# No tile operation left to POOL in the second block's preparation, and the head norms' sums taken two columns later

## The chip, the core and the metric

The kernel runs on one core of a Trainium2 chip. The metric is the device time of one execution in microseconds (us), the median of three runs. The engines are PE (TensorE: matmuls, and PEld its weight loads), DVE (VectorE), ACT (ScalarE), POOL (GpSimd) and SP (SyncE, which here only issues DMAs). Each works through its own instructions in order and waits on semaphores for the others.

## The reference, cut to what matters

Two network blocks run on 512 tokens of width 1024. The first has a gated linear recurrence, a conformer convolution, cross attention and feed-forward layers. The second is where the change lies: a projection of the normalized input to 43 columns of 128 features, a bidirectional RWKV recurrence, attention over a neighbourhood, and a mixture of experts.

```python
h = rmsnorm(x, norm1_g[l])
p = h @ w_in[l]
p_rwkv, q, k, v, gate_logits = jnp.split(p, IN_SPLITS, axis=-1)
y_a = rwkv7_bidirectional(p_rwkv, ...) @ w_o_rwkv[l]
y_b = neighbourhood_attention_2d(q, k, v, ...) @ w_o_na[l]
...
# inside the recurrence
kk = kk * lax.rsqrt(jnp.sum(kk * kk, axis=-1, keepdims=True) + 1e-12)
k_f = heads(k * (1.0 + (a_f - 1.0) * k_a))
bonus = jnp.sum(r_h * (k_f + k_b) * r_k, axis=-1, keepdims=True) * v_h
# inside the attention, for q and for k
t32 * lax.rsqrt(jnp.mean(t32 * t32, axis=-1, keepdims=True) + RMS_EPS) * g
```

## The kernel before

**Products and weights.** A float32 product is made of three matmuls on fp32r parts (`mm3`, L524 to L526): high weight times high and low input, low weight times high input. The weights arrive as 1 MB tiles (`raw`), and `Stream.piece` splits a quarter tile at a time: ACT copies the high part to `whi` (L353), and another engine subtracts it from `raw` to give `wlo` (L356). One piece holds four blocks of 128 by 128, so twelve matmuls. There are eight `whi` and eight `wlo` buffers. In the first block L356 runs on DVE. In `second_mixer` the `rest` engine is POOL, and `LOV = (0, 2)` keeps pieces 0 and 2 of each tile on DVE, so every second piece goes to POOL.

**Columns.** `columns` makes the 43 columns in the order `W_IN`, each from 8 blocks, that is 24 matmuls into one accumulator (`acc`, five of them). DVE takes a column out of it: L1235 with L1237 and L1239 for the recurrence's columns (r, k, v), L1287 for the attention's q, k and v (columns 15 to 26), L1295 for the gates. For the four k columns of the recurrence (`sums`) and the eight q and k columns of the attention (`nsums`) `collect` squares the result on ACT (L1250), and four matmuls of PE add the squares up by head (`by_head`, L648), with a copy by ACT (L1260). That sum stands one column behind: after the first half (`begin`) of the next column.

**Preparation.** `prep` runs for the four pairs of heads p = 0 to 3. For each of the two directions d, `decay` (L1447 to L1463) makes decays with two matmuls, a scan on DVE (L1457) and exponentials on ACT (L1461, L1462). `products` then makes `kf` (ACT L1472, then L1474) and the tile `ab` of four products: L1477, L1478, L1483 and L1481, with L1480 ahead of the last. POOL has L1474 and L1477, DVE the others. `gram` is 16 small matmuls a half on `ab` (L1496). Between the two grams L1522 adds the two directions' `kf` on POOL. POOL also issues the DMAs of L1546.

**What sets the order.** The generators of `columns`, `prep` and `inverse` are drawn in turn by tables of digits (PREP, INVS, SOLVE and others), and a scheduler then lays each engine's instructions in one fixed order. `inverse(0)`, a forward substitution of 62 short DVE operations (L1568, L1571), is drawn among the preparation of p = 2 and 3, and `inverse(1)` behind it among the gates' columns (the solve stage). The recurrence itself (`chunk`) and the first output product follow in the chunk stage.

Of the kernel before, what the change touches and what calls it, by code (L numbers as in the profile page):

```python
# [8 lines left out]
F32 = mybir.dt.float32  # L9
# [17 lines left out]
E = 32  # L27
# [1 line left out]
TG, TN = 22, 8  # L29
QS = ('sync', 'gpsimd')  # L30
INV = 2
LOV = (0, 2)
AHD = 2
ENDS, ENDL = (), (3, 5, 6, 7)
PREP = "1011101111000230011101111011111111211112"
# [13 lines left out]
FETCH, LOOK, NP = 0, 8, 4  # L49
# [278 lines left out]
class Stream:  # L328
# [3 lines left out]
    def __init__(self, tc, pool, src, first=0):  # L332
        self.tc, self.nc, self.src = tc, tc.nc, src
        nc = tc.nc
        self.raws, self.parts = [(pool, 2)], [(pool, 2 * NP)]
        self.c, self.s, self.raw, self.got = first, 0, {}, {}
        self.queue, self.rest, self.byv = nc.sync, nc.vector, ()

    def fetch(self, c):
        if c not in self.raw and c < len(CHUNKS):  # L340
# [4 lines left out]
    def piece(self, h):  # L345
        if h in self.got or h >= NP * len(CHUNKS):
            return
        self.fetch(h // NP)
        n = 2048 // NP
        raw = self.raw[h // NP][:, h % NP * n:(h % NP + 1) * n]  # L350
        pool, bufs = self.parts[h % len(self.parts)]
        hi = pool.tile([P, n], F32R, name="whi", bufs=bufs)
        self.nc.scalar.copy(hi, raw)  # L353
        lo = pool.tile([P, n], F32R, name="wlo", bufs=bufs)
        rest = self.nc.vector if h % NP in self.byv else self.rest
        rest.tensor_sub(lo, raw, hi.bitcast(F32))  # L356
        self.got[h] = (hi, lo)

    def load(self, c):
# [85 lines left out]
class Kernel:  # L445
# [758 lines left out]
    def columns(self):  # L1204


        nc = self.nc
        R = self.R
        xs, rb = self.final_norm()
        for i in range(DT):  # L1210
            self.put(f"x{i}", self.x[i])
        c0 = R.tile([P, 15], F32, name="c0")
        nc.vector.tensor_add(c0, self.v("mu_prev_2", 0, 15), self.v("mu_next_2", 0, 15))
        nc.vector.tensor_scalar(c0, c0, -1.0, 1.0, op0=ALU.mult, op1=ALU.add)
        begun = {}

        def begin(m):

            if ("w_in_2", 0, 0, m) not in self.done:
                begun[m] = self.acc()  # L1220
                for k in range(4):
                    self.mm3(begun[m], self.st.block("w_in_2", 0, k, m), xs[k], k == 0, False)

        def col(m):
            if m not in begun:
                return self.dense(xs, "w_in_2", 0, range(8), m)
            for k in range(4, 8):
                self.mm3(begun[m], self.st.block("w_in_2", 0, k, m), xs[k], False, k == 7)
            return begun.pop(m)

        def shifted(m, dst):
            h, a = self.tmp(2), self.tmp()
            nc.vector.memset(h[:, 0:1], 0.0)
            nc.vector.memset(h[:, S + 1:S + 2], 0.0)
            nc.vector.tensor_mul(h[:, 1:S + 1], col(m), rb)  # L1235
            nc.scalar.activation(a, h[:, 1:S + 1], AF.Copy, scale=c0[:, m:m + 1])
            nc.vector.scalar_tensor_tensor(a, h[:, :S], self.v("mu_prev_2", m), a, op0=ALU.mult,  # L1237
                                           op1=ALU.add)
            nc.vector.scalar_tensor_tensor(dst, h[:, 2:], self.v("mu_next_2", m), a, op0=ALU.mult,  # L1239
                                           op1=ALU.add)  # L1240
            return dst

        kept = {}
        sums = R.tile([P, 64], F32, name="sums")
        self.nsums = self.B.tile([P, 128], F32, name="nsums")

        def collect(t, to, at, scale=1.0):

            sq = self.tmp()
            nc.scalar.activation(sq, t, AF.Square, scale=scale)  # L1250
            return sq, to, at

        def columns():
            late = None
            for m in W_IN:
                begin(m)
                if late:
                    sq, to, at = late
                    late = None
                    nc.scalar.copy(to[:, 8 * at:8 * at + 8], self.by_head(sq))  # L1260
                    if to is sums and at == 3:
                        self.rk = self.rsqrts(sums, 32, [(slice(0, 32), 1.0, 1e-12)])
                    elif at == 7:

                        self.rn = self.rsqrts(self.nsums, 64, [(slice(0, 32), 1.0, 64 * EPS),
                                                               (slice(32, 64), 1.0 / 64, EPS)])
                yield
                if m < 12:
                    n, i = "rkv"[m // 4], m % 4
                    at = i if n == "k" else 4 + "rv".index(n) + 2 * (i % 2)  # L1270
                    kept[n, i] = shifted(m, self.x[at])
                    if n == "k":
                        late = collect(kept[n, i], sums, i, self.v("k_k_2", i))
                elif m == 12:
                    w = shifted(m, self.tmp())
                    self.wl = R.tile([P, S], F32, name="wl")
                    nc.scalar.activation(self.wl, w, AF.Tanh)
                elif m == 13:
                    self.al = shifted(m, R.tile([P, S], F32, name="al"))
                elif m == 14:  # L1280
                    g = shifted(m, self.tmp())
                    nc.scalar.activation(g, g, AF.Tanh, scale=0.5)
                    nc.vector.tensor_scalar(g, g, 0.5, 0.5, op0=ALU.mult, op1=ALU.add)
                    self.put("gl", g, nc.scalar)
                elif m < 27:
                    t, ps = self.tmp(), col(m)
                    nc.vector.tensor_mul(t.rearrange("p (c r) -> p r c", r=8),  # L1287
                                         ps.rearrange("p (r c) -> p r c", r=8),
                                         rb.rearrange("p (r c) -> p r c", r=8))
                    self.put("n%s%d" % ("qkv"[(m - 15) // 4], (m - 15) % 4), t)  # L1290
                    if m < 23:
                        late = collect(t, self.nsums, m - 15)
                else:
                    t = self.tmp()
                    nc.vector.tensor_mul(t, col(m), rb)  # L1295

                    nc.scalar.activation(t, t, AF.Tanh, bias=self.hg[:, m - 27:m - 26], scale=0.5)
                    self.put(f"gate{m - 27}", t, nc.scalar)
                yield

        todo = columns()
        for _ in range(2 * W_IN.index(8) + 2):
            next(todo)
        inv = iter(())
        at = 0
        for p in range(4):
            for _ in self.prep(p, *(kept[x, p] for x in "krv")):
                for g, n in ((inv, INVS), (todo, PREP)):
                    for _ in range(int(n[at])):
                        next(g, None)  # L1310
                at += 1
            if p == 1:
                inv = self.inverse(0)
        for _ in inv:
            pass
        near = self.neighbours()
        for n, _ in enumerate(self.inverse(1)):
            for g, at in ((todo, SOLVE), (near, NEAR)):
                for _ in range(int(at[n])):
                    next(g, None)  # L1320
        return todo, near
# [102 lines left out]
    def prep(self, p, k, r, v):  # L1424

        nc = self.nc
        R, T, M = self.R, self.tmp, self.M
        rev = lambda t, d: t[:, ::-1] if d else t
        by = lambda t: t.rearrange("p (c s) -> p c s", s=64)
        lo, up = HALF  # L1430
# [11 lines left out]
        decays, rates, kd, abs_ = [], [], [], []  # L1442
# [24 lines left out]
        def products(d):  # L1467

            E, I = decays[d]
            ta = rates[d]  # L1470
            kf = T()
            nc.scalar.activation(kf, ta, AF.Identity, bias=self.ka[:, 4 + p:5 + p],  # L1472
                                 scale=self.ka[:, p:p + 1])
            nc.gpsimd.tensor_mul(kf, kf, k)  # L1474
            kd.append(kf)
            ab = self.B.tile([P, 8, 320], F32, name="ab", bufs=2)
            nc.gpsimd.tensor_mul(ab[:, :, 192:256], by(rev(r, d)), E[:, :, 1:])  # L1477
            nc.vector.scalar_tensor_tensor(ab[:, :, P:192], by(rev(kk, d)), -1.0, E[:, :, :64],  # L1478
                                           op0=ALU.mult, op1=ALU.mult)
            nc.vector.scalar_tensor_tensor(ta, ta, 1.0, kk, op0=ALU.add, op1=ALU.mult)  # L1480
# [38 lines left out]
        gram(0)  # L1519
        yield  # L1520
        rr = T()
        nc.gpsimd.tensor_add(rr, kd[0], kd[1])  # L1522
        nc.vector.scalar_tensor_tensor(rr, rr, self.v("r_k_2", p), r, op0=ALU.mult, op1=ALU.mult)
        yield
        gram(1)
# [7 lines left out]
        for d in range(2):  # L1533
# [7 lines left out]
            t = T()  # L1541
# [203 lines left out]

    def second_mixer(self):
        nc = self.nc
        self.st.queue, self.st.rest, self.st.byv = nc.sync, nc.gpsimd, LOV
        self.q1, self.q2 = (getattr(nc, q) for q in QS)
        with self.tc.tile_pool(name="systems", bufs=1) as G, \  # L1750
                self.tc.tile_pool(name="both", bufs=1) as self.B:
# [19 lines left out]
            with self.tc.tile_pool(name="chunks", bufs=1) as self.R:  # L1771
# [28 lines left out]
                    next(out)  # L1800
                for _ in out:
                    pass
        self.st.queue, self.st.rest = nc.sync, nc.vector
        for i in range(DT):
            self.get(f"x{i}", self.x[i])

# [414 lines left out]
```

## Time and profile before

| | us |
|---|---|
| median of three runs | 2491.69 (2486.46 to 2494.93) |
| the profiled execution's own time | 2489.94 |
| its span in the profile | 2488.1 |
| PE busy in the span | 2378.5 (96%) |
| DVE busy | 1399.0 (56%) |
| ACT busy | 938.6 (38%) |
| POOL busy | 454.9 (18%) |

The span is the time from the first to the last instruction of the profiled execution, and 1.8 us of its own time lie around it. Stretches are named by us from the span's start: the second block's columns begin at about 1530, `prep` runs from about 1604 to 1784, the solve stage to 1876, and the chunk stage to 2062. Matmuls are pipelined and the profile models their ends, so that PE is shown busy a little longer than it is: a wait of PE is better read from the idle time ahead of a row, and its speed from the distance of two starts.

### The profile page before, as it was taken

Reading aid. Unit: us, or ns where it says so; the run is one execution under the profiler, and the core shown is the slowest. Engines: PE = TensorE matmul, PEld = TensorE weight load, DVE = VectorE, ACT = ScalarE, POOL = GpSimd, SP = SyncE. Lnnn points to the kernel's source line nnn. Section 1 sums busy time; section 2 is a strip of 40 time slices with the busy share of each in tenths; the row PEclk is TensorE's granted clock in tenths of the full one; section 3 lists DMA queues with packets and bytes.
Section 4 is the critical chain, followed back from the end, with each engine's and each line's share of the span. In section 5 each row is a group of like instructions: output and inputs, shape, how many; then the busy total and the mean of one; then the engine's idle time right before and its main releaser. Section 6 shows DMA issues by size and latency. Waiting matters only on the chain. (4 is left out here: it accounts for less than half of the span.)

```text
span 2488.1 us, 34872 instructions
## 1 busy us (share of the span) xinstructions
PE 2378.5 (96%) x13357; PEld 1845.1 (74%) x13357; DVE 1399.0 (56%) x2639; ACT 938.6 (38%) x1706; POOL 454.9 (18%) x428
## 2 busy tenths in 40 slices
PE   7999999999999999999999999988999989999996
PEld 6887788888888779888888888766876666764442
DVE  7998666545454546565645455669465776631110
ACT  4666444333243235444424244454243322321110
POOL 2012101101011000101101013344223221402211
PEclk8999999999999998999999999999898989989999
DMA  4332212222332213213222223355653434479998
GB/s 176 119 127 93 88 63 92 102 96 90 102 106 89 93 52 136 85 60 102 93 94 102 102 87 113 117 153 146 179 165 119 132 111 144 135 264 365 379 377 293
DMA packets 131197, 344.53 MB, mean 138 GB/s; under 512 B 40435, under 2 KB 66834, under 8 KB 101328
## 3 DMA queue, kind: packets, MB, share of 16 engines
q1 hardware_dynamic: 122944, 327.29, 38.2%
q0 software_dynamic: 5632, 10.49, 2.3%
q10 hardware_dynamic: 2448, 4.46, 0.5%
q8 instruction: 107, 1.75, 0.3%
q14 instruction: 66, 0.54, 0.1%
HBM read 307.33 MB, written 34.87 MB: 138 GB/s over the span
## 5 line engine op out<-in xcount | busy, mean ns | idle before, releaser
L524 PE MATMUL acc<-xn,whi 128*128 128x512 f32 x1656 | 660.9, 399 | 12.7 <-ACT xn L562 6.6
L353 ACT CAST whi<-raw 128x512 fp32r<-128x512 f32 x652 | 398.2, 620 | 708.0 <-PE acc L525 597.1
L526 PE MATMUL acc<-xn,wlo 128*128 128x512 f32 x1656 | 653.2, 395 | 1.6 <-DVE wlo L356 1.6
L525 PE MATMUL acc<-xn,whi 128*128 128x512 f32 x1656 | 654.0, 395 | 0.0
L356 DVE TENSOR_TENSOR wlo<-raw,whi 128x512 fp32r<-128x512 f32 x605 | 448.2, 746 | 294.6 <-ACT whi L353 292.5
L524 PEld LDWEIGHTS acc<-xn,whi 128*128 128x128 f32 x1656 | 314.9, 190 | 84.4 <-ACT xn L562 6.6
L526 PEld LDWEIGHTS acc<-xn,wlo 128*128 128x128 f32 x1656 | 314.4, 190 | 69.6 <-DVE wlo L356 2.4
L525 PEld LDWEIGHTS acc<-xn,whi 128*128 128x128 f32 x1656 | 315.2, 190 | 68.1 <-issue 3.4
L524 PE MATMUL acc<-act,whi 128*128 128x512 f32 (+1 forms) x676 | 252.9, 375 | 3.0 <-DVE tmp L1817 1.7
L525 PE MATMUL acc<-act,whi 128*128 128x512 f32 (+1 forms) x676 | 252.7, 374 | 2.6 <-DVE act L560 2.6
L526 PE MATMUL acc<-act,wlo 128*128 128x512 f32 (+1 forms) x676 | 252.8, 374 | 0.0
L723 POOL TENSOR_TENSOR tmp<-tmp 128x512 f32<-128x512 f32 x48 | 74.4, 1549 | 622.8 <-DVE tmp L721 555.7
L582 POOL TENSOR_TENSOR tmp<-tmp 128x512 f32<-128x512 f32 x56 | 80.6, 1440 | 421.7 <-ACT tmp L575 401.9
L524 PEld LDWEIGHTS acc<-act,whi 128*128 128x128 f32 x676 | 130.0, 192 | 25.8 <-DVE tmp L1817 2.2
L525 PEld LDWEIGHTS acc<-act,whi 128*128 128x128 f32 x676 | 130.2, 193 | 25.2 <-DVE act L560 3.0
L526 PEld LDWEIGHTS acc<-act,wlo 128*128 128x128 f32 x676 | 130.1, 192 | 21.9
L560 DVE TENSOR_TENSOR act<-tmp,act 128x512 fp32r<-128x512 f32 x88 | 61.1, 694 | 89.4 <-ACT act L559 87.5
L559 ACT CAST act<-tmp 128x512 fp32r<-128x512 f32 x88 | 54.3, 620 | 122.1 <-POOL tmp L723 91.3
L2099 POOL DMA_INDIRECT out<-tmp,tid x32 | 50.7, 1583 | 245.0 <-ACT tmp L2098 155.4
L356 POOL TENSOR_TENSOR wlo<-raw,whi 128x512 fp32r<-128x512 f32 x47 | 66.7, 1422 | 133.3 <-ACT whi L353 105.0
L703 DVE SCALAR_TENSOR_TENSOR tmp<-tmp,vec 128x512 f32<-128x512 f32 x96 | 72.2, 752 | 17.0 <-ACT tmp L700 15.3
L2067 PE MATMUL acc<-raw,xn 128*64 128x512 f32 x320 | 75.8, 602 | 4.3 <-DMA raw<-wex 4.2
(439 smaller groups left out, 3290.4 us busy)
## 6 DMA issues: line engine op xcount, KB each, us to landing
raw<-wst SPq DMA_DIRECT2D x162, 1024.0 KB, 5.0
raw<-wex SPq DMA_DIRECT2D x56, 1024.0 KB, 16.5
whi<-wex SPq DMA_DIRECT2D x56, 256.0 KB, 6.5
wlo<-wex SPq DMA_DIRECT2D x56, 256.0 KB, 6.3
x<-wex SPq DMA_DIRECT2D x12, 1024.0 KB, 9.6
bkv<-bkv SPq DMA_DIRECT2D x32, 192.0 KB, 2.7
rec<-ab SPq DMA_DIRECT2D x8, 512.0 KB, 3.2
sp_gate<-tmp ACTq DMA_DIRECT2D x16, 256.0 KB, 2.6
```

The source lines that it names most:

```text
L353: self.nc.scalar.copy(hi, raw)
L356: rest.tensor_sub(lo, raw, hi.bitcast(F32))
L524: nc.tensor.matmul(ps, w[0], x[0], start=first, stop=False)
L525: nc.tensor.matmul(ps, w[0], x[1], start=False, stop=False)
L526: nc.tensor.matmul(ps, w[1], x[0], start=False, stop=last)
L559: nc.scalar.copy(h, src)
L560: nc.vector.tensor_sub(lo, src, h.bitcast(F32))
L582: nc.gpsimd.tensor_add(n, accs.pop(), t)
L703: nc.vector.scalar_tensor_tensor(z, h[:, k:k + S], taps[k], y, op0=ALU.mult, op1=ALU.add)
L723: nc.gpsimd.tensor_mul(z, u, ge)
L2067: nc.tensor.matmul(pg[a], h[:, o:o + SLOTS], w[2 * k + n], start=c + k == 0, stop=c + k == 4)
L2099: nc.gpsimd.indirect_dma_start(out=self.out[hf], out_offset=bass.IndirectOffsetOnAxis(ap=tid[:, i:i + 1], axis=0), in_=y, in_offset=None, ...
```

## The change

The split of every weight piece, both products of POOL in `products` and the sum of the two `kf` go to DVE. The table LOV and the switch of engines in `Stream` go. The list `late` in `columns` now holds up to two entries: sums of the recurrence's k columns are still taken behind the next column, and those of the attention's q and k when a second one is waiting, or beyond column 22.

```diff
@@ class Stream
-        self.queue, self.rest, self.byv = nc.sync, nc.vector, ()
+        self.queue = nc.sync
...
-        rest = self.nc.vector if h % NP in self.byv else self.rest
-        rest.tensor_sub(lo, raw, hi.bitcast(F32))
+        self.nc.vector.tensor_sub(lo, raw, hi.bitcast(F32))
@@ columns
-            late = None
+            late = []
             for m in W_IN:
                 begin(m)
-                if late:
-                    sq, to, at = late
-                    late = None
+                if late and (late[0][1] is sums or len(late) > 1 or m > 22):
+                    sq, to, at = late.pop(0)
                     nc.scalar.copy(to[:, 8 * at:8 * at + 8], self.by_head(sq))
...
-                        late = collect(kept[n, i], sums, i, self.v("k_k_2", i))
+                        late.append(collect(kept[n, i], sums, i, self.v("k_k_2", i)))
...
-                        late = collect(t, self.nsums, m - 15)
+                        late.append(collect(t, self.nsums, m - 15))
@@ prep
-            nc.gpsimd.tensor_mul(kf, kf, k)
+            nc.vector.tensor_mul(kf, kf, k)
...
-            nc.gpsimd.tensor_mul(ab[:, :, 192:256], by(rev(r, d)), E[:, :, 1:])
+            nc.vector.tensor_mul(ab[:, :, 192:256], by(rev(r, d)), E[:, :, 1:])
...
-        nc.gpsimd.tensor_add(rr, kd[0], kd[1])
+        nc.vector.tensor_add(rr, kd[0], kd[1])
@@ second_mixer
-        self.st.queue, self.st.rest, self.st.byv = nc.sync, nc.gpsimd, LOV
+        self.st.queue = nc.sync
```

Line numbers fall by one to three in the changed kernel: L356 becomes L354, L648 L646, L1287 L1284, L1474 L1471, L1477 L1474, L1478 L1475, L1480 L1477, L1481 L1478, L1483 L1480, L1496 L1493.

On DVE, in `products` for p = 1, from the weight piece that stands in the scan's place to the end of the first direction's products, this is the order before:

```order
L356 TENSOR_TENSOR wlo<-raw,whi 128x512
L1457 SCALAR_TENSOR_TENSOR tmp<-cst,tmp 128x512
L1460 MEMSET tmp 128x8
L1478 SCALAR_TENSOR_TENSOR ab<-tmp 128x8x64 x2
L1480 SCALAR_TENSOR_TENSOR tmp<-tmp 128x512
L1483 TENSOR_TENSOR ab<-tmp 128x8x64
L1481 SCALAR_TENSOR_TENSOR ab<-tmp 128x8x64
```

And this is the same stretch now:

```order
L354 TENSOR_TENSOR wlo<-raw,whi 128x512
L1474 TENSOR_TENSOR ab<-x_106,tmp 128x8x64
L1475 SCALAR_TENSOR_TENSOR ab<-tmp 128x8x64
L1471 TENSOR_TENSOR tmp<-tmp,x_99 128x512
L1477 SCALAR_TENSOR_TENSOR tmp<-tmp 128x512
L1480 TENSOR_TENSOR ab<-tmp 128x8x64
L1478 SCALAR_TENSOR_TENSOR ab<-tmp 128x8x64
```

The scan and the first direction's L1474 and L1475 now stand ahead of these rows; in all, the first gram of p = 1 has two L1474 and one L1471 more ahead of it on DVE.

On PE, in the preparation of p = 2, the third of the attention's sums (its square is tmp_14096) stands here before, followed by the first gram:

```order
L524 MATMUL acc_14114<-xn_12758,whi_14041 128x512
L525 MATMUL acc_14114<-xn_12759,whi_14041 128x512
L526 MATMUL acc_14114<-xn_12758,wlo_14043 128x512
L648 MATMUL aux_14131<-cst_80,tmp_14096 128x2 x4
L1496 MATMUL aux_14137<-ab_14060 64x64
```

In the changed kernel the second sum (of tmp_13814) stands in that place, with four matmuls of the column between it and the gram:

```order
L522 MATMUL acc_14108<-xn_12758,whi_14035 128x512
L523 MATMUL acc_14108<-xn_12759,whi_14035 128x512
L524 MATMUL acc_14108<-xn_12758,wlo_14037 128x512
L646 MATMUL aux_14125<-cst_80,tmp_13814 128x2 x4
L522 MATMUL acc_14108<-xn_12762,whi_14071 128x512
L523 MATMUL acc_14108<-xn_12763,whi_14071 128x512
L524 MATMUL acc_14108<-xn_12762,wlo_14073 128x512
L522 MATMUL acc_14108<-xn_12766,whi_14071 128x512
L1493 MATMUL aux_14131<-ab_14054 64x64
```

The third sum moved to the place that the fourth has before, a column of 24 matmuls later; each of the eight has moved to the place of the next one in this way. Ahead of the first gram itself PE has, from the first decay matmul of its pair, 46, 34, 26 and 49 column matmuls for p = 0 to 3, where it had 44, 24, 29 and 38.

On DVE, in the same preparation, the column out of which that third square is made (L1287) stands behind the products of the first direction before, with the rows of the substitution (z, NT) between:

```order
L1478 SCALAR_TENSOR_TENSOR ab_14101<-tmp_13979,tmp_14029 128x8x64
L1568 TENSOR_TENSOR z_14070<-X_13996,NT_13997 128x135
L1480 SCALAR_TENSOR_TENSOR tmp_13986<-tmp_13986,tmp_13979 128x512
L1483 TENSOR_TENSOR ab_14060<-tmp_14057,tmp_13989 128x8x64
L1481 SCALAR_TENSOR_TENSOR ab_14060<-tmp_13986,tmp_13989 128x8x64
L1571 TENSOR_TENSOR NT_13997<-NT_13997,z_14070 128x5x27
L1287 TENSOR_TENSOR tmp_14076<-acc_14040,rb_13012 128x8x64
```

Now it stands ahead of them:

```order
L1284 TENSOR_TENSOR tmp_14070<-acc_14034,rb_13012 128x8x64
L1568 TENSOR_TENSOR NT_13991<-NT_13991,z_14031 128x4x28
L1471 TENSOR_TENSOR tmp_14051<-tmp_14051,x0_99 128x512
L1477 SCALAR_TENSOR_TENSOR tmp_13980<-tmp_13980,tmp_13973 128x512
L1480 TENSOR_TENSOR ab_14054<-tmp_14051,tmp_13983 128x8x64
L1478 SCALAR_TENSOR_TENSOR ab_14054<-tmp_13980,tmp_13983 128x8x64
```

So the column leaves its accumulator before the first direction's products, and these now hold L1471 as a row of DVE's own.

## Rows read from the trace of the kernel before

**Rows 1.** Stretches: us, then busy time (and instructions) by engine, PEclk, DMA.
```profile
1604.00:1639.00 35.00, 31.41 (x194) 23.07 (x193) 26.80 (x55) 20.23 (x38) 15.38 (x14) 0.95 0.51 125
1639.00:1681.00 42.00, 35.80 (x209) 27.47 (x209) 25.51 (x38) 19.16 (x37) 19.07 (x21) 0.92 0.55 152
1681.00:1725.00 44.00, 38.71 (x224) 29.58 (x224) 40.82 (x70) 18.79 (x38) 19.79 (x18) 0.88 0.48 119
1725.00:1784.00 59.00, 55.18 (x350) 43.30 (x349) 35.86 (x64) 17.36 (x36) 13.29 (x9) 0.94 0.72 203
1784.00:1876.00 92.00, 88.03 (x782) 72.22 (x780) 59.52 (x131) 36.29 (x72) 25.32 (x29) 0.87 0.49 148
1876.00:2062.00 186.00, 171.43 (x2136) 121.49 (x2137) 126.37 (x406) 58.05 (x182) 56.58 (x128) 0.94 0.38 119
```
**Rows 2.** Waits of PE, 1600 to 1784: us in total, times, longest us.
```profile
PE aux L648 <- ACT tmp L1250: 9.1, 2, 5.3
PE aux L1496 <- DVE ab L1481: 8.7, 2, 6.2
PE aux L660 <- DVE tmp L1460: 1.1, 1, 1.1
```
**Rows 3.** PE in order of time: start, us, instruction, [idle before <- what ended it].
```profile
1655.74 1.97 PE L1496 MATMUL aux<-ab 64*64 64x64 f32 x32 [6.20 <-DVE ab L1481]
...
1659.08 0.63 PE L524 MATMUL acc<-xn,whi 128*128 128x512 f32 x1
...
1659.51 0.63 PE L525 MATMUL acc<-xn,whi 128*128 128x512 f32 x1
...
1663.52 0.39 PE L524 MATMUL acc<-xn,whi 128*128 128x512 f32 x1
...
1663.75 0.39 PE L525 MATMUL acc<-xn,whi 128*128 128x512 f32 x1
...
1698.37 1.87 PE L648 MATMUL aux<-cst,tmp 128*128 128x2 f32 x8 [5.29 <-ACT tmp L1250]
```
**Rows 4.** DVE in order of time, in the products of p = 1.
```profile
1644.25 0.73 DVE L1510 SCALAR_TENSOR_TENSOR tmp<-x,vec,aux 128x512 f32<-128x512 f32 x1
...
1645.23 1.68 DVE L356 TENSOR_TENSOR wlo<-raw,whi 128x512 fp32r<-128x512 f32 x1
...
1649.46 1.57 DVE L1480 SCALAR_TENSOR_TENSOR tmp<-tmp 128x512 f32<-128x512 f32 x1
1652.19 1.73 DVE L1483 TENSOR_TENSOR ab<-tmp 128x512 f32<-128x512 f32 x1 [1.16 <-POOL tmp L1474]
1653.85 1.75 DVE L1481 SCALAR_TENSOR_TENSOR ab<-tmp 128x512 f32<-128x512 f32 x1
1655.51 0.68 DVE L1480 SCALAR_TENSOR_TENSOR tmp<-tmp 128x512 f32<-128x512 f32 x1
1656.12 0.68 DVE L1483 TENSOR_TENSOR ab<-tmp 128x512 f32<-128x512 f32 x1
```
**Rows 5.** POOL in order of time, in the same stretch.
```profile
1650.44 2.94 POOL L1474 TENSOR_TENSOR tmp<-tmp,x 128x512 f32<-128x512 f32 x2
1653.34 1.71 POOL L356 TENSOR_TENSOR wlo<-raw,whi 128x512 fp32r<-128x512 f32 x1
```
**Rows 6.** DVE in order of time, in the preparation of p = 2.
```profile
1685.09 0.74 DVE L1510 SCALAR_TENSOR_TENSOR tmp<-x,vec,aux 128x512 f32<-128x512 f32 x1
...
1690.84 1.68 DVE L356 TENSOR_TENSOR wlo<-raw,whi 128x512 fp32r<-128x512 f32 x1
...
1696.53 1.06 DVE L1287 TENSOR_TENSOR tmp<-acc,rb 128x512 f32<-128x512 f32 x1
```
**Rows 7.** Waits of PE, 1530 to 1606.
```profile
PE aux L592 <- POOL tmp L582: 1.1, 1, 1.1
```
**Rows 8.** Groups of instructions by line, POOL, 1530 to 2130: count | busy us, mean ns | idle before.
```profile
L356 POOL TENSOR_TENSOR wlo<-raw,whi 128x512 fp32r<-128x512 f32 x47 | 66.7, 1422 | 133.3 <-ACT whi L353 105.0 <-issue 12.3 <-PE acc L526 10.8
```
**Rows 9.** Waits of ACT, 1530 to 2130.
```profile
ACT whi L353 <- PE acc L525: 79.9, 44, 8.0
```

More of the change, by code (lines that the diff above doesn't have):

```diff
@@ L31 @@
 INV = 2
-LOV = (0, 2)
 AHD = 2
@@ L1802, in second_mixer @@
                     pass
-        self.st.queue, self.st.rest = nc.sync, nc.vector
+        self.st.queue = nc.sync
         for i in range(DT):
```

## The prediction

> **What bounds the kernel now.** I read the stretches first. PE is the bound nearly everywhere, but in the preparation it has holes: 31.41 of 35 us busy, 35.80 of 42, 38.71 of 44 and 55.18 of 59 in the four pairs' stretches, and there the granted clock falls to 0.95, 0.92, 0.88 and 0.94 [rows 1]. Next, the waits of PE say who makes the holes: 9.1 us in two waits of L648 for a square of ACT, and 8.7 us in two waits of a gram (L1496) for the last product of DVE; the longest are 5.3 and 6.2, so the others are 3.8 and 2.5, together 17.8 us [rows 2]. The square itself waits for DVE's L1287, so all four are DVE being late. Then the clock: after the 6.20 us wait two matmuls start 0.43 us apart, a little later 0.23 us [rows 3]; these are the levels of 1.2 and 2.4 GHz. In the four stretches (1 - clock) times length is 1.75 + 3.36 + 5.28 + 3.54 = 13.9 us, so 27.9 us at the low level. About 5 us of these lay inside the waits themselves (my reading of 3.0 in the third, and less in the others); the rest costs (0.43 - 0.23) / 0.43 of itself, 10.6 us at most. I take 9, since the small matmuls of the grams do not double. The preparation thus loses some 27 us on PE.
>
> Last, why DVE is late. In the products of p = 1 one and the same operation takes 1.57, 1.73 and 1.75 us while POOL is at L1474 and L356, and 0.68 just after, when POOL is idle; L1483 also stands idle for 1.16 us until POOL's L1474 is done [rows 4, 5]. So a DVE operation on two tiles of SBUF loses about 1.0 us to a POOL operation beside it. The Trainium skill (page SBUF — State Buffer, section Who interferes with whom) has a DVE instruction with two SBUF inputs and a GpSimd instruction that reads SBUF exclude each other, so that the second waits for the whole of the first; the trace agrees in kind, with 1.75 us against 0.68.
>
> **The change, part by part.** *Work moved.* POOL has 47 weight splits of 1422 ns [rows 8]; by the code 8 + 8 products and 4 sums come with them. On DVE each costs the distance of two starts, 1656.12 - 1655.51 = 0.61 us [rows 4]: 67 x 0.61 = 40.9 us more DVE work, spread from 1530 to 2062. In the preparation it is 36 of them (16 splits and all 20 others), 22 us. Against that stand the 1.0 us stretches, which go wherever DVE was busy beside POOL.
>
> *Second pair (wait of 6.2).* From L1510 at 1644.25 to the end of the last product at 1655.60 DVE took 11.35 us [rows 4]. Without POOL it loses 1.00 (L356), 0.89 (L1480), 1.16 (the wait), 1.05 (L1483) and 1.07 (L1481), 5.17 in all; the order adds two L1474 and one L1471, 1.83. It ends 3.3 us earlier, at 1652.25. PE was there at 1655.74 - 6.20 = 1649.54 [rows 3] and has ten matmuls more ahead of the gram now (34 against 24), 2.27 us: 1651.8. The wait left is 0.45.
>
> *First pair (2.5).* The same count: three stretched products back (about 3), one product added (0.6), two matmuls more (0.45). 0.3 is left.
>
> *Third pair (5.3).* The sum is now a column later, 24 x 0.227 = 5.4 us of PE work, and its column is taken out ahead of the products, so its wait goes altogether. What is late next is the first gram, which stood right behind. PE would be there at 1698.37 - 5.29 = 1693.08 [rows 3], less three matmuls (26 against 29) plus the sum's own work, about 1693.3. DVE before had done the products just ahead of L1287 at 1696.53 [rows 6]. Four rows between 1685.09 and there are stretched by about 1.0 each (the split at 1690.84 is one [rows 6]); L1474, L1471 and L1287 (0.9) come in ahead and one L1478 goes. That is 1696.4 - 4.1 + 1.5 = 1693.8 at best; the substitution's rows stand among them and may be hit, so I take 1695. The wait left is 1.5, and 0.5 at the second gram: 2.
>
> *Fourth pair (3.8).* Again the sum's wait goes. DVE's run to the first products holds three operations more and the substitution's middle rows; PE has 11 matmuls more ahead (49 against 38), 2.5 us. DVE is the slower here by my count of the order with the distances above, by about 3 us.
>
> So 17.8 becomes 0.3 + 0.45 + 2 + 3, about 5.8: 12.0 us back. Of the clock's 9 I leave 3, since waits of 2 to 3 us may again be followed by a low clock, as the 2.5 us one was (0.95 in its stretch [rows 1]): 6 back. The wait for rk (L660, 1.1 [rows 2]) stays.
>
> *Columns before the preparation.* PE waits 1.1 us for the last sum of the norm on POOL [rows 7]; two splits that stood among those sums are gone from POOL, so this goes: 1.0 back.
>
> *Splits as a wait.* A split on DVE can stand behind a run of products. But ACT's L353 waits 79.9 us in 44 times for PE's L525 to free a buffer [rows 9]: the pieces are made as far ahead as eight buffers allow, and one piece is 12 x 0.227 = 2.7 us of PE work. A delay of 10 us is covered; with a run of products of over 15 us it would not be.
>
> *Solve and chunk stage.* 12 and 8 splits move there, 7.3 and 4.9 us of DVE. In the solve stage PE is busy 88.03 of 92 [rows 1] and the stretches lost offset the new work; in the chunk stage DVE is on the recurrence's path, but POOL, which also copies and scales state there, loses 8 pieces of 1.4. Bounds: 2 us gained, and 5 lost (all eight on the path). I take 1 lost, near the middle.
>
> Sum: -12.0 - 6 - 1.0 + 1 = -18 us on the profiled execution's 2489.94, that is 2472. The median of the runs is 1.75 higher, so the forecast is 2474.
>
> **The rivals.** *All waits go.* If the scheduler's order meets the products in time in the third and fourth pair too, 17.8 + 9 + 1.1 come back, -28: 2464. For it: DVE's 40.82 of 44 us in the third pair are swollen by the stretches [rows 1]. Against: the grams there stand early in PE's order.
>
> *The wait comes back at the grams.* DVE is busy 40.82 of 44 us there already, and gets 22 us of work in the preparation. If the stretches are only half as large as I read them, some 10 us of it are net, and they lie ahead of grams. The sums' waits then go (9.1), the grams' grow by about as much, and the clock gains 2 or 3 less: -6 instead of -18, 2486. The Trainium skill (page Perfetto Trace Analysis, section Optimizing Scalar/DVE Operations) speaks for this one: with DVE saturated it would move work off it, though it adds that DVE and GpSimd share a read port, so that this might not help; the rows of the trace bear out the second half.
>
> *Slower: DVE becomes the bound.* If POOL's operations took their time in the shadow of DVE's own waits, so that the stretches bring back under 10 us, DVE runs 12 us or more behind at the end of the preparation. It then carries this into the solve stage, where the splits (12 of them) lie in one queue with 62 dependent rows of `inverse(1)`: pieces come late, PE waits for `wlo`, and the clock, 0.87 there already [rows 1], falls further. 12 for the backlog and 5 for the chunk stage, less 8 for sums and front, is +9: 2501. It decides when DVE in the stretches of the preparation is busy without a gap; it had 2 to 23 us of gaps in each [rows 1].
>
> *No effect.* The sums one column later are no use if their squares are later by as much. With L1287 ahead of the products in the order, I hold this for covered by the case of the grams.
>
> **How the numbers follow.** Forecast 2474 (from 2466 to 2481): 0.56. All waits gone, 2464: 0.17. Waits back at the grams, 2486: 0.20. Slower, 2501: 0.07. A measurement of this kernel tells about 0.3%, 7.5 us, from no change. Faster by more than that, under 2484, is the first two and a fifth of the third: 0.77; within it, the rest of the third: 0.16; slower 0.07. The range leaves out the slower case and a part of the fastest: 2462 to 2488.
>
> **What would show it.** Right: no operation of DVE on 128x512 tiles over about 1.1 us between 1604 and the gates; DVE busy in the four preparation stretches about as long as before, in spite of 36 more operations; L648 gone from PE's waits; the waits of L1496 under 6 us together and now in p = 2 and 3; granted clock over 0.95 in the third stretch; the solve stage some 20 us earlier. Wrong: PE waiting for `wlo`, or for L1496 by more than 10 us, or a preparation (L1447 of p = 0 to the last L1540) that is not at least 12 us shorter. A longer chunk stage than 186 us by over 5 would show that the splits lie on the recurrence's path.

## The result and the profile after

| | before | after |
|---|---|---|
| median of the runs (4 each) | 2489.07 us (2483.7 to 2494.93) | 2453.38 us (2450.2 to 2466.59) |
| the profiled execution's own time | 2489.94 | 2453.04 |
| its span | 2488.1 | 2451.3 |

The ratio is 0.986, with a 95% interval of 0.984 to 0.988: 35.7 us less by the medians, 36.9 by the two profiled executions. The forecast was 18 less, 2474, with a range of 2462 to 2488. The sign and the mechanism were right; the size was half of what came, and the range did not hold the time.

The first lines of the page of the changed kernel:

```profile
span 2451.3 us, 34809 instructions
...
PE 2359.5 (96%) x13357; PEld 1830.2 (75%) x13357; DVE 1403.8 (57%) x2706; ACT 938.1 (38%) x1706; POOL 359.6 (15%) x361
```

DVE has 67 operations more than before (2706 against 2639) and is busy only 4.8 us longer (1403.8 against 1399.0). POOL has 67 fewer and is busy 95 us less.

**Where the 36.8 us of span lie.** I followed single instructions of PE through both traces. The 7201st matmul stands in the columns ahead of the first wait that differs: it starts at 1560.0 us before and at 1553.6 after. These 6.4 us lie in work that the change does not touch. In the profiled executions of the kernels below, which all share that work, the same matmul starts at 1552.1 to 1560.0, so the 6.4 are scatter, and the execution of before was at its late end. (With one profile of each kernel, whether the medians' 35.7 hold more than the 32.2 and this scatter cannot be told.) From that matmul to the first L1646 of the recurrence (L1643 now), through the rest of the columns, the preparation and the solve stage, before took 316.4 us and after 284.2: **32.2 us less**. From there to the end it is 1.8 us more. This middle stretch holds 1963 or 1964 instructions of PE in every kernel, and I use it below to compare them. These are its busy times by engine, in the kernel before and then in the changed one (columns as in [rows 1]):

```profile
1560.00:1876.40 316.40, 290.64 (x1964) 230.46 (x1962) 217.64 (x418) 127.68 (x245) 107.56 (x100) 0.92 0.53 152
```

```profile
1553.60:1837.80 284.20, 280.97 (x1963) 223.40 (x1961) 211.81 (x471) 127.84 (x245) 26.22 (x44) 0.95 0.58 168
```

DVE does 53 operations more in 5.8 us less. Idle time of PE, the stretch less PE's busy time, was 25.8 us and is 3.2. The time at the low level of the clock, 2 x (1 - clock) x length, was 51 us and is 28. The four stretches of the preparation and the solve and chunk stages, which answer to [rows 1], are:

```profile
1595.60:1624.00 28.40, 28.28 (x182) 20.40 (x181) 26.86 (x64) 19.64 (x36) 0.78 (x1) 1.00 0.51 125
1624.00:1659.20 35.20, 34.94 (x215) 26.24 (x214) 26.99 (x52) 19.58 (x37) 9.47 (x16) 1.00 0.79 219
1659.20:1697.20 38.00, 37.81 (x247) 28.06 (x245) 34.91 (x77) 21.43 (x44) 4.91 (x8) 1.00 0.62 166
1697.20:1746.00 48.80, 48.80 (x332) 39.49 (x329) 31.36 (x74) 14.42 (x30) 0.00 (x0) 1.00 0.77 210
1746.00:1837.40 91.40, 89.15 (x782) 73.50 (x781) 60.84 (x144) 37.13 (x72) 7.31 (x16) 0.85 0.49 151
1837.40:2023.20 185.80, 168.83 (x2139) 119.63 (x2140) 131.38 (x412) 58.01 (x182) 47.58 (x120) 0.96 0.39 120
```

In the preparation PE now has no hole to speak of, and its clock is granted in full: the 0.95, 0.92, 0.88 and 0.94 of before are 1.00 four times. The waits of PE within the middle stretch, which answer to [rows 2] and [rows 7] (us in total, times, longest):

```profile
PE aux L1396 <- ACT tmp L1391: 1.4, 2, 0.7
PE aux L1493 <- DVE ab L1478: 0.5, 2, 0.3
```

The 17.8 us of [rows 2] for the sums and the grams have become 0.5, and the wait for rk and those ahead of the preparation are gone. The first line is the solve stage's. Not listed is the wait that ends the stretch, ahead of the first L1643: it is 1.3 us, and was 1.4.

This is DVE in the products of p = 1, which answers to [rows 4]:

```profile
1629.49 0.75 DVE L1507 SCALAR_TENSOR_TENSOR tmp<-x,vec,aux 128x512 f32<-128x512 f32 x1 [0.95 <-DMA bkv<-tmp]
...
1634.94 0.69 DVE L1471 TENSOR_TENSOR tmp<-tmp,x 128x512 f32<-128x512 f32 x1
1635.54 0.69 DVE L1477 SCALAR_TENSOR_TENSOR tmp<-tmp 128x512 f32<-128x512 f32 x1
1636.14 0.69 DVE L1480 TENSOR_TENSOR ab<-tmp 128x512 f32<-128x512 f32 x1
1636.74 0.68 DVE L1478 SCALAR_TENSOR_TENSOR ab<-tmp 128x512 f32<-128x512 f32 x1
```

Every product takes 0.68 or 0.69 us, where [rows 4] has 1.57 to 1.75, and they follow each other at 0.60. From the start of L1507 (L1510 before) to the end of the last product it is 7.93 us, against 11.35.

### The profile page after: what moved, and what is told of

It is laid out like the page before. It is cut to its first block, busy times and chain, and to the rows that moved or that the text cites. A ratio compares the mean times of both kernels' runs of the same rounds, so it can differ in the third digit from the quotient of the medians.

```text
span 2451.3 us, 34809 instructions
## 1 busy us (share of the span) xinstructions
PE 2359.5 (96%) x13357; PEld 1830.2 (75%) x13357; DVE 1403.8 (57%) x2706; ACT 938.1 (38%) x1706; POOL 359.6 (15%) x361
## 3 DMA queue, kind: packets, MB, share of 16 engines
q8 instruction: 107, 1.75, 0.3%
## 5 line engine op out<-in xcount | busy, mean ns | idle before, releaser
L354 DVE TENSOR_TENSOR wlo<-raw,whi 128x512 fp32r<-128x512 f32 x652 | 479.9, 742 | 307.3 <-ACT whi L352 304.3
L701 DVE SCALAR_TENSOR_TENSOR tmp<-tmp,vec 128x512 f32<-128x512 f32 x96 | 72.2, 752 | 17.0 <-ACT tmp L698 15.3
L684 DVE TENSOR_TENSOR x<-x,acc 128x512 f32<-128x512 f32 x80 | 52.2, 681 | 39.5 <-PE acc L524 39.5
```

The lines of the kernel that those rows point to most:

```text
L354: self.nc.vector.tensor_sub(lo, raw, hi.bitcast(F32))
L684: self.nc.vector.tensor_add(self.x[m], self.x[m], ps)
L701: nc.vector.scalar_tensor_tensor(z, h[:, k:k + S], taps[k], y, op0=ALU.mult, op1=ALU.add)
```

## The experiments

The theory (A) was that DVE came late because an operation of it on two SBUF tiles is held up by a POOL operation beside it, and that the rest followed from that. The first four kernels take the change apart, the next three put POOL or DVE work back without any use, and the last one tries the same step elsewhere.

| kernel | median, us | ratio to before (95%) | middle stretch, us | PE idle in it, us | low clock in it, us |
|---|---|---|---|---|---|
| before | 2489 | | 316.4 | 25.8 | 51 |
| after | 2453.38 | 0.984 to 0.988 | 284.2 | 3.2 | 28 |
| e1_move: engines only | 2452.18 | 0.983 to 0.987 | 283.8 | 3.1 | 28 |
| e2_late: sums only | 2489.06 | 0.998 to 1.002 | 317.9 | 28.4 | 48 |
| e3_splits: sums and splits | 2475.87 | 0.992 to 0.996 | 304.1 | 15.3 | 48 |
| e4_products: sums and products | 2473.03 | 0.991 to 0.995 | 303.0 | 15.8 | 38 |
| e5_pool_extra | 2458.20 | 0.985 to 0.990 | 289.4 | 7.7 | 30 |
| e8_pool_triple | 2473.46 | 0.992 to 0.995 | 302.2 | 16.9 | 37 |
| e7_dve_extra | 2458.26 | 0.986 to 0.989 | 289.6 | 4.5 | 37 |
| e9_state | 2458.29 | 0.986 to 0.990 | 284.5 | 3.4 | 28 |

The middle stretch is read to 0.1 us, from one profiled execution of each kernel. The changed kernel and e9, which do the same work there, differ by 0.3 us, so it tells more than a median where intervals overlap. The low clock is the sum of the trace's stretches at 0.5.

**Engines only (e1_move).** The changed kernel, with the sums one column behind again:

```diff
-                if late and (late[0][1] is sums or len(late) > 1 or m > 22):
+                if late:
```

> The changed kernel with the sums of the attention's q and k taken one column behind, as before: only the moves from POOL to DVE are left. Theory A (DVE was late because its operations were stretched beside POOL and waited for POOL's product; the place of the sums matters little once that is gone): the squares of the third and fourth pair come 4 to 6 us earlier, the waits of L646 in the preparation are under 2 us together, all waits of PE there under 4 us, median within 5 us of the changed kernel, 2454 to 2459. Theory B (the two sums of 9.1 us had to be moved; engines alone mend only the first two pairs): 7 to 9 us of waits of L646 stay, with 4 us or more of low clock, median 2465 to 2472.

2452.18 us, and one wait in the preparation:

```profile
PE aux L1493 <- DVE ab L1478: 0.3, 1, 0.3
```

Theory A holds, B falls: the move of the engines, with the order that the scheduler lays for it, is the whole gain. With DVE on time the square of the fresh column is there when its sum's turn comes: in the preparation of p = 2 L1284 starts at 1672.30 and takes 1.14 us, and the sum follows at 1674.16 without a wait. The second column of distance (the sums stand two columns behind, one more than before) has nothing left to do. The order is a part of this: here too L1284 stands ahead of the first direction's products, as in the changed kernel, and no run has the engines moved in the old order.

**Sums only (e2_late).** The kernel before, with the list of two entries and nothing moved to DVE.

> The kernel before with the sums two columns behind and nothing moved: the splits, products and the kf sum stay on POOL. Theory A: the waits of the grams of the first two pairs stay (8.7 us), the sums' 9.1 us go, but the grams right behind them in pairs three and four find DVE still stretched and wait 5 to 8 us; with the low clock the gain is small, median 2478 to 2490 against 2489 before. Theory B: 9.1 us of waits and about 4.5 of low clock go, median 2473 to 2477.

2489.06 us, no change. The waits of PE in the middle stretch:

```profile
PE aux L1495 <- DVE ab L1480: 19.8, 5, 6.6
...
PE aux L648 <- ACT tmp L1250: 0.8, 1, 0.8
```

Before, the grams had 8.7 us and the sums 9.1 [rows 2]; now the grams (L1495 here) have 19.8, more than the 8.7 and 5 to 8 that I expected. A consumer that is taken later hands its wait to the next consumer of the same late engine. This is what the rival "the wait comes back at the grams" of the prediction foretold, but it belongs to this half of the change alone, and for another reason: there it was the added work of DVE, and here DVE has none.

**Only the splits, only the products (e3_splits, e4_products).** Both have the sums two columns behind. In e3 the three POOL operations of `prep` stay on POOL; in e4 they go to DVE, and the 47 splits stay.

```diff
-            nc.gpsimd.tensor_mul(kf, kf, k)
+            nc.vector.tensor_mul(kf, kf, k)
...
-            nc.gpsimd.tensor_mul(ab[:, :, 192:256], by(rev(r, d)), E[:, :, 1:])
+            nc.vector.tensor_mul(ab[:, :, 192:256], by(rev(r, d)), E[:, :, 1:])
...
-        nc.gpsimd.tensor_add(rr, kd[0], kd[1])
+        nc.vector.tensor_add(rr, kd[0], kd[1])
```

> The changed kernel with L1471, L1474 and L1519 (kf, ab and the kf sum) back on POOL: only the 47 splits are moved, with the sums two columns behind. Theory A, with the losses of the two kinds of operations adding up: 2 of 5 us per pair come back, waits of PE in the preparation 5 to 10 us, median 2462 to 2470. Theory C (what counts is the explicit wait of L1480 for POOL's product, not the stretching): the waits of grams stay at 8 us or more and appear in all four pairs, median 2472 to 2482.

> The kernel before with the sums two columns behind and the products and the kf sum on DVE: the 47 splits stay on POOL. Theory A, adding up: 3 of 5 us per pair come back, operations of 1.7 us on DVE remain beside the splits, waits of PE in the preparation 4 to 8 us, median 2459 to 2467. Theory C: nothing waits for POOL any more on the way to the grams, waits under 2 us, median within 4 us of the changed kernel, 2453 to 2458.

Both came out slower than theory A's numbers, e3 within C's and e4 outside both. In the preparation of e3 PE waits for grams alone, in all four pairs:

```profile
PE aux L1493 <- DVE ab L1478: 12.6, 4, 4.7
```

In e4 the grams' waits are small, as expected, and others have come up, among them two in the solve stage for a weight piece that DVE split too late. On the way to these splits four short rows of `inverse(1)` take 1.29 to 1.43 us beside POOL's splits, the next ones 0.34 to 0.38:

```profile
PE aux L1495 <- DVE ab L1480: 3.1, 3, 1.3
PE acc L526 <- DVE wlo L356: 2.3, 2, 1.4
```

PE's idle time nearly adds up: e3 takes away 25.8 - 15.3 = 10.5 us, e4 10.0, together 20.5, and the whole change 22.6. So the splits and the products weigh about the same. Theory C's numbers fit e3 and not e4: if waiting for POOL's product were all, e4 would have the whole gain, and it has less than half. The times do not add up: 12.3 + 13.4 = 25.7 of 32.2 us. About 3 of the missing 6.5 are the clock, by estimate: e3 keeps 48 us of low clock and e4 38, so they gain 3 and 13 of the 23 that the whole gains, and a microsecond at the low level loses about (0.43 - 0.23) / 0.43 of itself [rows 3]. 2 more are idle time of PE, and the rest stays open.

**Idle work on POOL (e5_pool_extra, e8_pool_triple).** The changed kernel, with one product more on POOL behind each L1474, or three, whose result nobody reads. In e5 the order of DVE, PE and ACT is row for row that of the changed kernel; in e8 it differs in some rows of p = 1, where L1474 and L1475 of the second direction stand later. Nobody waits for the new operations.

```diff
+        idle = R.tile([P, S], F32, name="idle")
...
             nc.vector.tensor_mul(ab[:, :, 192:256], by(rev(r, d)), E[:, :, 1:])
+            nc.gpsimd.tensor_mul(by(idle), ab[:, :, 192:256], E[:, :, 1:])
```

> The changed kernel with eight idle products more on POOL: behind each L1474 POOL multiplies its result by E into a tile that nobody reads. The order of DVE and PE is that of the changed kernel, and nobody waits for the new operations. Theory A (a DVE operation on two tiles of SBUF loses about 1.0 us to each POOL operation beside it): the first gram of each pair comes up to 2 us later, less what is spare (nothing in pairs two and three, 1.0 in pair four); waits of PE 4 to 7 us, perhaps 2 to 6 us of low clock, the preparation 158 to 166 us instead of 153.4, median 2458 to 2466. Theory D (the long rows of DVE came from its waits for POOL's results, not from POOL's work beside it): the preparation within 1 us of 153.4, median within 4 us of 2453.

> The same with three idle products behind each L1474, so 24, which is as much POOL work as the preparation had before. Theory A: six stretches a pair, the first grams 5 to 6 us late in all four pairs, 18 to 23 us of waits and 6 to 9 of low clock, the preparation 175 to 186 us, so about the 182.4 of the kernel before, median 2475 to 2486, although DVE and PE do what they do in the changed kernel. Theory D: within 1 us of 153.4.

The preparation is 158.3 and 171.4 us by the rule of the expectations (first decay matmul to the last transpose), against 153.4; so theory A, not D, with e5 at the low end and e8 below it. These are DVE and POOL of e5 in p = 1 (lines two higher than in the changed kernel):

```profile
1630.55 0.42 DVE L1452 TENSOR_SCALAR tmp<-tmp 128x512 f32<-128x512 f32 x1
1630.88 1.67 DVE L1477 SCALAR_TENSOR_TENSOR ab<-tmp 128x512 f32<-128x512 f32 x1
...
1635.11 0.69 DVE L1477 SCALAR_TENSOR_TENSOR ab<-tmp 128x512 f32<-128x512 f32 x1
1635.71 1.69 DVE L1472 TENSOR_TENSOR tmp<-tmp,x 128x512 f32<-128x512 f32 x1
```

```profile
1630.78 1.23 POOL L1476 TENSOR_TENSOR idle<-ab,tmp 128x512 f32<-128x512 f32 x1 [1.63 <-DVE ab L1475]
1635.34 1.52 POOL L1476 TENSOR_TENSOR idle<-ab,tmp 128x512 f32<-128x512 f32 x1 [3.33 <-DVE ab L1475]
```

Both POOL operations hold up the one DVE operation that comes to them. So do four more of the eight; in the other two it is mostly POOL that waits (3.28 us at 1614.86 and 4.81 at 1675.39). The two shown delay the gram of p = 1, whose wait was 0.3 us and is 1.4, and PE's waits for grams are 4.3 us in all:

```profile
PE aux L1495 <- DVE ab L1480: 4.3, 4, 1.4
```

In e8 they are 10.3, against the 18 to 23 that I expected. I had taken every idle product for 1.0 us. By the busy time of DVE in the middle stretch it is less:

```profile
1553.00:1842.40 289.40, 281.72 (x1964) 224.08 (x1963) 217.86 (x471) 127.71 (x245) 43.43 (x52) 0.95 0.57 165
```

```profile
1560.00:1862.20 302.20, 285.31 (x1964) 226.15 (x1962) 229.41 (x471) 127.59 (x245) 66.46 (x68) 0.94 0.55 158
```

e5 has (217.86 - 211.81) / 8 = 0.76 us for each, e8 (229.41 - 211.81) / 24 = 0.73, with the same 471 operations of DVE. e8's 18 us are more than half of the 32.2 that the change brought. Its 24 products took POOL 40.0 us; the preparation before had 51.5 us of POOL more than now (68.7 against 17.2).

**The same idle work on DVE (e7_dve_extra).** `nc.vector` instead of `nc.gpsimd` in the line of e5.

> The changed kernel with eight idle products more on DVE instead, at the same place of the program (the fixed order of DVE shifts somewhat with them). By theory A an operation on DVE costs it 0.61 us and stretches nothing, so that eight cost less than the same eight on POOL: up to 1.2 us a pair, 2 to 5 us of waits, the preparation 154 to 159 us, median 2453 to 2459. If DVE is at its limit in the preparation (the rival of the prediction in which the waits return at the grams) it is 5 us or more, with low clock behind it: 160 or more.

```profile
1558.10:1847.70 289.60, 285.06 (x1963) 226.42 (x1962) 217.45 (x479) 127.54 (x245) 26.10 (x44) 0.94 0.57 165
```

DVE is busy (217.45 - 211.81) / 8 = 0.70 us longer for each. **A product left on POOL cost DVE 0.73 to 0.76 us, the same product on DVE 0.70.** On time e7 is no cheaper than e5 (289.6 and 289.4 us), at the edge of what I expected, and for another reason: PE waits for one gram only (1.8 us), but its clock falls to 0.50 for 10.2 us at 1705, 60 us behind that wait and with no other in between. The order had drawn both decays of p = 3 together. PE there:

```profile
1701.68 1.12 PE L1445 MATMUL aux<-wl,wup 64*128 64x512 f32 x2
1702.65 1.02 PE L1449 MATMUL aux<-al,wup 64*128 64x512 f32 x2
1703.60 1.05 PE L646 MATMUL aux<-cst,tmp 128*128 128x2 f32 x8
1704.58 1.59 PE L658 MATMUL aux<-cst,sums 128*64 128x128 f32 x16
1706.10 2.07 PE L1445 MATMUL aux<-wl,wup 64*128 64x512 f32 x2
1707.97 1.91 PE L1449 MATMUL aux<-al,wup 64*128 64x512 f32 x2
```

The pair of L1445 takes 1.12 us, and 2.07 a little later: the clock fell in a run of matmuls that are narrow or use half of the array's rows, with PE never idle. This is one instance; no run shows that the run of matmuls is the cause.

**The same step elsewhere (e9_state).** L1666, the decay of the state in the chunk stage, 56 operations, from POOL to DVE too.

```diff
-EB = 'g'
+EB = 'v'
```

> The changed kernel with the 56 small products of the state by the decay (L1666, POOL, 421 ns each) on DVE too. In the chunk stage DVE's own rows read PSUM and are as long beside POOL as alone (277 and 284 ns for L1694), so theory A has nothing to give back there: the chunk stage stays at 192 to 200 us, median within 4 us of 2453. If POOL beside DVE were a cost by itself anywhere, the chunk stage would gain 5 us or more, under 191.

2458.29 us, and the chunk stage (first L1643 to the last L1707) 198.5 us against 196.1. Nothing came back where DVE's rows read PSUM: L1694 has a median of 284 ns in both. The difference to the changed kernel is within the intervals.

## Why the prediction was right in kind and half in size

*The bound and the mechanism* were right. DVE being late to the grams and sums was what PE waited for, and POOL beside DVE was why. e5 and e8 show it, e5 with the order of DVE, PE and ACT unchanged: idle POOL work alone takes back 5.2 and 18.0 of the 32.2 us. How the rest divides between DVE's own waits for POOL's product and the new order, no run separates.

*What failed* is the size of terms. The forecast left 5.8 us of the four waits, 1.1 for rk and 3 of low clock in the preparation; measured were 0.5, none and none. It took 1 us lost behind the preparation, where 1.7 came back.

The terms of the sum, by its own steps:

| step | forecast | measured |
|---|---|---|
| wait of the first pair | 2.5 to 0.3 | to 0 |
| second pair | 6.2 to 0.45 | to 0.3 |
| third pair | 5.3 to 2 | to 0.2 |
| fourth pair | 3.8 to 3 | to 0 |
| wait for rk | stays, 1.1 | gone |
| low clock in the preparation | 9 to 3 | to 0 |
| waits ahead of the preparation | -1.0 | -2.5 |
| solve and chunk stage | +1 | waits of the solve stage -1.7, chunk 0 |

*The second pair* was the model case. The forecast had DVE at the last product 8.0 us after its L1510, worked out row by row; it was 7.93.

*The third pair* failed by a cushion. The same count gave "1693.8 at best", 8.7 us after L1510; I took 1695 because the substitution's rows "may be hit". They were not: no tile operation was left on POOL, and they took 0.18 to 0.29 us. It took 8.35 us, from 1663.29 to 1671.64, and the gram followed at once:

```profile
1671.79 1.15 PE L1493 MATMUL aux<-ab 64*64 64x64 f32 x32 [0.19 <-DVE ab L1478]
```

*The fourth pair* is the step with the wrong sign. I had DVE "the slower here", "by about 3 us"; the last product that the gram reads (L1478) ended at 1707.78 and the gram started at 1708.78, so DVE had 1.0 us to spare, an error of 4. The prediction does not show this count row by row, so which row made it too late stays open. It does not mention what POOL had taken from the substitution's own rows, on the way there. The two groups of the middle stretch, in the kernel before and in the changed one:

```profile
L1568 DVE TENSOR_TENSOR z<-X,NT 128x31 f32<-128x31 f32 (+15 forms) x62 | 27.9, 451 | 1.3
L1571 DVE TENSOR_TENSOR NT<-NT,z 128x31 f32<-128x31 f32 (+15 forms) x62 | 27.7, 446 | 1.2
```

```profile
L1565 DVE TENSOR_TENSOR z<-X,NT 128x31 f32<-128x31 f32 (+15 forms) x62 | 20.9, 338 | 0.7
L1568 DVE TENSOR_TENSOR NT<-NT,z 128x31 f32<-128x31 f32 (+15 forms) x62 | 20.9, 338 | 0.6
```

124 short operations gave back 13.8 us, more than the eight L1481 and L1483 together (18.3 to 11.0). Of these, 7.5 are `inverse(0)`'s, among the preparation of p = 2 and 3 (28.5 to 21.0), the rest `inverse(1)`'s in the solve stage. My count of 1.0 us a hit was about right for one hit; apart from two of the four stretched rows in the third pair (1.28 and 1.34 us in the trace of before) I had not counted how many there were.

*The wait for rk* was to stay, without a reason given. It was one more such hit: the last row of its chain, L641 (L639 now), stood beside a split on POOL. Before, DVE and POOL, and now DVE:

```profile
1612.26 1.22 DVE L641 SCALAR_TENSOR_TENSOR sums<-tmp,sums 128x32 f32<-128x32 f32 x1
```

```profile
1612.17 1.26 POOL L356 TENSOR_TENSOR wlo<-raw,whi 128x512 fp32r<-128x512 f32 x1 [7.10 <-ACT whi L353]
```

```profile
1603.69 0.17 DVE L639 SCALAR_TENSOR_TENSOR sums<-tmp,sums 128x32 f32<-128x32 f32 x1
```

*The clock.* Since the waits went altogether, none was left to be followed by a low clock, and 32.2 - 22.6 = 9.6 us came back beside the idle time, where I had 6. Waits of 2 to 3 us would indeed have been a risk, though not a sure one: in e3 those of 1.95 and 2.67 us came with 6.8 and 3.4 us of low clock, in e8 one of 2.07 with none. Waits of 0.7 to 1.4 in the preparation of e4 and e5 were followed by none.

*The sums.* "Its wait goes altogether", put down to the second column of distance, was the right outcome, but the distance was not needed: e1 has it with one column. In e2 the distance alone takes the sums' waits away too, the grams take them over, and nothing is gained.

*Ahead of the preparation* I counted one wait of 1.1 us [rows 7]; a wait of 0.8 for a sum and one of 0.6 for `wl` went with it. *In the solve stage* the waits of L1399 halved (2.7 to 1.4 us, L1396 now) and one of 0.3 went. The splits on DVE made no piece late: no wait for `wlo` is left, and the slower rival did not come near.

So what came was the rival "all waits go", which stood at 2464 and a chance of 0.17. With the waits around the preparation it is 32.2 us instead of its 28, 2457.7 from the profiled execution, and with the 6.4 us of scatter in the first block less and 1.8 of the end more, 2453. *The range* ended 2 us under the rival's own centre, although single runs of the kernel before scatter by 5 us to either side of the median: it left no room for that scatter on top of the likeliest rival.

The Trainium skill (page SBUF — State Buffer, section Who interferes with whom) has the order of issue decide which of DVE and GpSimd waits. The trace of e5 bears that out: at 1630.88 POOL had begun 0.10 us earlier, and DVE's row grew to 1.67; at 1614.86 POOL came into a run of DVE products and it was POOL that took 3.28 us, while they stayed at 0.69:

```profile
1614.86 3.28 POOL L1476 TENSOR_TENSOR idle<-ab,tmp 128x512 f32<-128x512 f32 x1 [7.28 <-DVE ab L1475]
```

## What to carry to other kernels

Work given to POOL was not free for DVE here: where DVE is busy with operations on two SBUF tiles, count every POOL operation beside it at about what the same operation would cost on DVE (0.73 to 0.76 against 0.70 us here, by the mean of 24 and 8), and look for DVE groups whose mean is well over their shortest row, short operations above all. Before a consumer is moved to dodge a wait, ask which consumer of the same producer stands next: it inherits the wait. And when a count from rows says "at best", a cushion on it needs a row of its own.

## What was not expected of the hardware

The scan, 1.22 us alone, took 2.10 beside POOL in e8, and L1452, an operation with a single SBUF input, 1.29 instead of 0.42. A row that has PSUM for one of its inputs did not grow:

```profile
1613.56 1.29 DVE L1452 TENSOR_SCALAR tmp<-tmp 128x512 f32<-128x512 f32 x1
...
1614.88 2.10 DVE L1455 TENSOR_TENSOR_SCAN tmp<-cst,tmp 128x512 f32<-128x512 f32 x1
...
1616.94 0.68 DVE L1233 TENSOR_TENSOR tmp<-acc,rb 128x512 f32<-128x512 f32 x1
```

POOL paid as well: the same product took 1.67 us on average in e8 and 2.12 in e5, and 1.23 at the shortest shown here. And PE's clock fell in e7 without a wait near it, in a run of narrow matmuls, so that a new order may cost clock even where no engine is late.
